# A full block of B21 and B22 in the pairs of chunks: from seventh to third place

## The chip, the cores and the metric

The kernel runs on one core of a Trainium2 chip. The metric is the device time of one execution in microseconds (us); before the change it is 2211.46 us, the median of three runs (2210.63 to 2211.67).

## The reference, cut to what matters

The program is a decoder of two layers on 256 positions of width 2048, all in float32. Each layer has attention, a SwiGLU feed-forward block and a gated embedding. The change is in the feed-forward block:

```python
D_MODEL = 2048; SEQ = 256
D_FF = 5632

def swiglu(h, w1, w3, w2):
    return (jax.nn.silu(h @ w1) * (h @ w3)) @ w2
...
x = x + swiglu(rmsnorm(x, g_ffn[i]), w1[i], w3[i], w2[i])
```

`h` is 256 x 2048, `w1` and `w3` are 2048 x 5632, `w2` is 5632 x 2048.

## The kernel before

**Products.** Every float32 operand is split into a high and a low part in a rounded format (`hi`, `lo` for weights, `st_hi`, `st_lo` for the turned input), and a product is three matmuls: hi by st_hi (L400), lo by st_hi (L401), hi by st_lo (L402). A weight block is loaded by a DMA of the SP queue into `raw` (L112) or, for the blocks spoken of here, into held tiles `r11`, `r12`, `r2` (L105). ScalarE then writes `hi` (L127) and VectorE writes `lo` (L128).

**The stream of blocks.** `WeightStream` keeps one list of all blocks in the order in which TensorE takes them. Each call of `next()` returns the next block and, ahead of that, splits blocks until three full ones are split from the place on; of the small ones only one at a time, since their parts `shi`, `slo` have one buffer each. The full parts have three buffers, so a split waits until TensorE is done with the third full block before it. Splits stay in order on ScalarE and on VectorE (L129 to L131). Behind the split of a small block come its `sums` (L134), additions of held tiles on VectorE, which make the operands of later small blocks. Loads are issued up to two places ahead (L116), each when its buffer is free.

**Pairs of chunks.** The feed-forward block goes over 11 pairs in each layer: a chunk of 512 columns of w1 and the same of w3, in groups of 3, 4 and 4 pairs; after each group its rows of w2 are multiplied. So there are 22 pairs in all, in six groups. The first four k-tiles of a pair are done by a scheme with fewer products (seven instead of eight, with sums of quarters A of the input and B of the weights), the other twelve plainly. A pair takes twelve blocks from the stream; they are named here as in the rest of the text. Small forms, 6 matmuls each: **p1** (B11), **p7** (with the form T3), **p5**, **p6** into `side` tiles, and **q** (the last part of c21). **R** is the full block of B21 and B22, read from `r2`: 6 matmuls into c11 and 6 into c12. Full blocks of four k-tiles, 24 matmuls each: **W1a, W1b, W1c** of w1 into c11 and c21, **W3a, W3b, W3c** of w3 into c12 and c22. The order before is

p1, W1a, p7, W1b, p5, W3a, R, W1c, p6, W3b, q, W3c.

**What else runs.** After p1 ScalarE copies it to `v1` (L493). After p6 VectorE makes v6, v7, v8 (L506 to L509). When c11 and c21 are done, it adds them (L630), ScalarE applies the sigmoid (L632) and VectorE multiplies (L633). When c12 and c22 are done, L636 and L637 run twice each, then two transposes (L325): this is called the tail. The turned result goes into the w2 input by four steps of four copies each, 16 copies `xt` of 32x256 on ScalarE (L330, four are called a move), and a split (`st_hi` L312, `st_lo` L313); these five steps are put off into a list and run one by one at the five calls of `work` inside the next pair (or inside the first w2 chunk, where a group ends). A pair that follows another in its group has them, the first of a group doesn't.

**Order.** Each engine has its own queue, whose order is fixed at compile time: by the order of the text among what that step takes to be ready. Where the trace departs from the text, the trace has the order that ran.

Of the kernel before, what the change touches and what calls it, by code (L numbers as in the profile page):

```python
# [38 lines left out]
CW = 512  # L39
# [4 lines left out]
SN = 2  # L44
# [112 lines left out]
def yoco_kernel(  # L157
# [17 lines left out]
    def cols(w, k0, nk, c0, n, step=4):  # L175

        return [Block(w[(k0 + k) * P:(k0 + min(k + step, nk)) * P, c0:c0 + n].rearrange("(a p) n -> p a n", p=P),
                      min(step, nk - k), n) for k in range(0, nk, step)]

    def pair_cols(wa, ca, wb, cb, nk):  # L180

        def at(w, k, c):
            return w[k * P:(k + SN) * P, c:c + CW].rearrange("(a p) n -> p a n", p=P)

        b11, b21, b12, b22 = at(wa, 0, ca), at(wa, SN, ca), at(wb, 0, cb), at(wb, SN, cb)
        rest = [cols(w, 2 * SN, nk - 2 * SN, c, CW) for w, c in ((wa, ca), (wb, cb))]
        def held(name, a=SN, **more):
            return Block(None, a, CW, held=name, unit=len(blocks), **more)

        return [held("r11", loads=[("r11", [b11])], sums=[("r11", "r12", 0), ("r12", "r2", 1)]), rest[0][0],  # L190
                held("r12", loads=[("r12", [b12]), ("r2", [b21, b22])]), rest[0][1],
                held("r11", sums=[("r11", "r2", 1)]), rest[1][0], held("r2", 2 * SN), rest[0][2],
                held("r11", sums=[("r11", "r2", 0)]), rest[1][1], held("r11"), rest[1][2]]

    IW = IDXN // 3
    FGROUPS = [(0, 3), (3, 7), (7, 11)]
# [27 lines left out]
    stream = WeightStream(tc, raw_pool, half_pool, blocks)  # L224
# [3 lines left out]
    first = const.tile([P, 1], F32, name="first")  # L228
# [76 lines left out]
    def new_station():  # L305
        return (station.tile([P, KT, S], F32R, tag="st_hi", name="st_hi"),
                station.tile([P, KT, S], F32R, tag="st_lo", name="st_lo"))
# [77 lines left out]
    def new_ss():  # L385
        return const.tile([P, NT, NC], F32, tag="ss", name="ss", bufs=2)
# [3 lines left out]
    def work(n):  # L390
        for _ in range(n):
            if bg:
                bg.popleft()()

    def products(st, o, kt, t, h, l, first, last):
        sl = slice(t * P, (t + 1) * P)
        return products_of(st[0][:, kt, sl], st[1][:, kt, sl], o, h, l, first, last)

    def products_of(sh, sl, o, h, l, first, last):
        nc.tensor.matmul(o, sh, h, start=first, stop=False)  # L400
        nc.tensor.matmul(o, sh, l, start=False, stop=False)  # L401
        return nc.tensor.matmul(o, sl, h, start=False, stop=last)  # L402

    def accumulate(st, ktiles, n, acc, pace=(), start=0, end=None, new=None, stop=(True, True)):


        block = 0
        done = start
        while done < (len(ktiles) if end is None else end):
            hi, lo, a = stream.next()  # L410
            for j in range(a):
                kt = ktiles[done + j]
                h, l = hi[:, j * n:(j + 1) * n], lo[:, j * n:(j + 1) * n]
                first, last = done + j == (0 if new is None else start), done + j == len(ktiles) - 1
                for t in range(NT):
                    end_ = products(st, acc[t][:, :n], kt, t, h, l, first and (new is None or new[t]), last and stop[t])
            done += a
            work(pace[block] if block < len(pace) else 0)
            block += 1
        return end_  # L420

    def new_acc():
        return [ps_acc.tile([P, CW], F32, tag="acc", name=f"acc{t}") for t in range(NT)]

    ALL = list(range(KT))
# [7 lines left out]
    class Forms:  # L433
# [20 lines left out]
        def of(self, i):  # L454
            return lambda j: (self.hi[:, i - 1, j, :], self.lo[:, i - 1, j, :])
# [11 lines left out]
    def pair_of_chunks(st, forms, nk, quad):  # L467


        c11, c21, c12, c22 = quad  # L470

        def tiles(k0, t):
            sl = slice(t * P, (t + 1) * P)
            return lambda j: (st[0][:, k0 + j, sl], st[1][:, k0 + j, sl])

        def form(o, of, alone, block=None, at=0):

            hi, lo, _ = stream.next() if block is None else block
            for j in range(SN):
                sl = slice((at + j) * CW, (at + j + 1) * CW)  # L480
                products_of(*of(j), o, hi[:, sl], lo[:, sl], alone in ("alone", "first") and j == 0,
                            alone in ("alone", "last") and j == SN - 1)

        def side_acc(i):
            if i < 2:
                return ps_at.tile([P, CW], F32, tag="at", name=f"side{i}")
            return ps_tr.tile([P, CW], F32, tag="tr", name=f"side{i}")

        ktiles = list(range(nk))
        p1, p5, p6, p7 = (side_acc(i) for i in (0, 2, 3, 1))  # L490
        v1, v6, v7, v8 = (forms.side(n) for n in ("v1", "v6", "v7", "v8"))
        form(p1, tiles(0, 0), "alone")
        nc.scalar.activation(v1, p1, AF.Copy)  # L493
        accumulate(st, ktiles, CW, (c11, c21), (1,), 2 * SN, 2 * SN + 4, new=(True, True))
        form(p7, forms.of(3), "alone")
        work(1)
        accumulate(st, ktiles, CW, (c11, c21), (1,), 2 * SN + 4, 2 * SN + 8)
        form(p5, forms.of(1), "alone")
        work(1)
        accumulate(st, ktiles, CW, (c12, c22), (1,), 2 * SN, 2 * SN + 4, new=(True, True))  # L500
        block = stream.next()
        form(c11, tiles(SN, 0), "more", block)
        form(c12, forms.of(4), "more", block, SN)
        accumulate(st, ktiles, CW, (c11, c21), (), 2 * SN + 8, stop=(True, False))
        form(p6, forms.of(2), "alone")
        nc.vector.tensor_add(v6, v1, p6)  # L506
        nc.vector.tensor_add(v7, v6, p7)
        nc.vector.tensor_sub(v6, v6, p5)
        nc.vector.tensor_sub(v8, v7, p5)  # L509
        accumulate(st, ktiles, CW, (c12, c22), (), 2 * SN + 4, 2 * SN + 8)  # L510
        form(c21, tiles(SN, 1), "last")
        return v1, v7, v6, v8

# [109 lines left out]
    def feed_forward(layer, st, forms, r, ss, nxt, scratch):  # L623
        for gi, (f0, f1) in enumerate(FGROUPS):
            hid = new_station()
            for f in range(f0, f1):
                quad = [ps_acc.tile([P, CW], F32, tag="acc", name=f"acc{j}") for j in range(4)]
                v = pair_of_chunks(st, forms, KT, quad)
                for t in range(NT):
                    nc.vector.tensor_add(v[t], v[t], quad[t])  # L630
                    sg = scratch.tile([P, CW], F32, tag="g", name="sg", bufs=1)
                    nc.scalar.activation(sg, v[t], AF.Sigmoid, scale=r[:, t:t + 1])  # L632
                    nc.vector.scalar_tensor_tensor(v[t], v[t], r[:, t:t + 1], sg, op0=ALU.mult, op1=ALU.mult)  # L633
                accumulate(st, ALL, CW, quad[2:], (), 2 * SN + 8)
                for t in range(NT):
                    nc.vector.tensor_sub(v[2 + t], quad[2 + t], v[2 + t])  # L636
                    nc.vector.scalar_tensor_tensor(v[2 + t], v[2 + t], r[:, t:t + 1], v[t], op0=ALU.mult, op1=ALU.mult)  # L637
                later = []
                ut = transposed_blocks(scratch, v[2:], moves=(1, 1), later=later)
                sl = (slice(None), slice(4 * (f - f0), 4 * (f - f0) + 4), slice(None))  # L640
                bg.extend(later)
                bg.append(lambda ut=ut, sl=sl: split(hid[0][sl], hid[1][sl], ut))
            last = gi == len(FGROUPS) - 1
            for c in range(NC):
                acc = new_acc()
                accumulate(hid, list(range(4 * (f1 - f0))), CW, acc, (3, 2) if c == 0 else ())
                for t in range(NT):
                    xs = x[t][:, c * CW:(c + 1) * CW]
                    nc.vector.tensor_add(xs, xs, acc[t])  # L649
                if last:  # L650
                    square_sum(ss, c, scratch)
                    nxt(c)
# [145 lines left out]
    st = new_station()  # L798
# [49 lines left out]
    with ExitStack() as outer:  # L848
# [3 lines left out]
        ss, st = new_ss(), new_station()  # L852
        forms = Forms(inner)
# [15 lines left out]
        ss, st = new_ss(), new_station()  # L869
# [4 lines left out]
    with tc.tile_pool(name="att1", bufs=1) as pool:  # L874
        kv_st, st = st, new_station()
# [21 lines left out]
    with ExitStack() as outer:  # L897
# [3 lines left out]
        ss, st = new_ss(), new_station()  # L901
        forms = Forms(inner)
# [65 lines left out]
```

## Time and profile before

| | before |
|---|---|
| median of three runs | 2211.46 us |
| profiled execution, its own time | 2210.84 us |
| span of the profiled execution | 2209.1 us |
| TensorE matmuls | 2177.4 us busy, 9780 matmuls |
| VectorE | 1629.6 us busy |
| ScalarE | 1313.7 us busy |
| moved by DMA | 419.23 MB, mean 190 GB/s |
| granted TensorE clock, mean | 0.999 |

How to read it: the span goes from the first to the last instruction of the profiled execution. Matmuls are pipelined and their ends are modelled, so a row of 0.39 us for a matmul overlaps the next one; what counts is the distance from start to start. An idle time is listed with what ended it ("idle before <-releaser").

### The profile page before, as it was taken

How to read it: one execution, taken by the hardware profiler on the slowest of the kernel's cores; microseconds unless marked ns; L12 is line 12 of the kernel's file. 1: busy time of each engine (PE TensorE's matmuls, PEld its weight loads, DVE VectorE, ACT ScalarE, POOL GpSimd, SP SyncE). 2: the span in 40 equal slices, each digit the busy share in tenths (PEclk: the TensorE clock that was granted, in tenths of full speed). 3: DMA queues.
4: the chain of work that ended last, by engine and by line, in shares of the span. 5: the costliest groups of instructions: out<-in, count | busy, mean ns of one | idle time of the engine just before them, and what ended most of it. 6: DMA issues, size and time to landing. Idle time of an engine off the chain costs nothing.

```text
span 2209.1 us, 24961 instructions
## 1 busy us (share of the span) xinstructions
PE 2177.4 (99%) x9780; PEld 1788.8 (81%) x9780; DVE 1629.6 (74%) x1706; ACT 1313.7 (59%) x1676; POOL 39.1 (2%) x38
## 2 busy tenths in 40 slices
PE   9999999999999999999999999999999999999998
PEld 8787788878878887888888778877888888878877
DVE  5877778866887578877777768886678756887764
ACT  5556676644665347666676657675366634676553
POOL 0110000000000000000000000000000000000000
PEclk9999999999999999999999999999999999999999
DMA  7564565656556555555566456556565566546553
GB/s 249 185 191 153 189 201 170 220 183 199 200 181 202 192 187 184 186 189 178 184 212 214 153 172 201 189 182 218 167 224 200 172 209 204 177 162 214 192 190 115
DMA packets 211382, 419.23 MB, mean 190 GB/s; under 512 B 7728, under 2 KB 14512, under 8 KB 211136
## 3 DMA queue, kind: packets, MB, share of 16 engines
q1 hardware_dynamic: 208400, 410.68, 56.1%
q0 software_dynamic: 1248, 4.27, 0.6%
q10 hardware_dynamic: 1616, 2.69, 0.4%
q8 instruction: 76, 1.25, 0.2%
q14 instruction: 42, 0.34, 0.0%
HBM read 415.48 MB, written 2.12 MB: 189 GB/s over the span
## 4 chain that ended last, share of the span: by engine, by line
PE 85%; ACT 7%; DVE 5%; issue 2%; DMA 0%; POOLq 0%; POOL 0%; DVEq 0%; ACTq 0%
PE acc L401 26%; PE acc L402 26%; PE acc L400 26%; ACT xt L330 3%; ACT hi L127 3%; DVE lo L128 2%; PE side L401 2%; PE side L402 1%; PE side L400 1%; PE ps_s L564 1%; PE ps_o L601 1%; DVE slo L128 1%; ACT shi L127 1%; DVE xt L332 1%; PE ps_p L592 0%
## 5 line engine op out<-in xcount | busy, mean ns | idle before, releaser
L400 PE MATMUL acc<-hi,st_hi 128*128 128x512 f32 (+2 forms) x2828 | 1093.0, 387 | 4.2 <-ACT st_hi L312 4.1
L401 PE MATMUL acc<-lo,st_hi 128*128 128x512 f32 (+2 forms) x2828 | 1090.6, 386 | 1.9 <-DVE lo L128 1.7
L402 PE MATMUL acc<-hi,st_lo 128*128 128x512 f32 (+2 forms) x2828 | 1089.1, 385 | 0.0
L128 DVE TENSOR_TENSOR lo<-raw,hi 128x2048 fp32r<-128x2048 f32 (+1 forms) x347 | 795.2, 2293 | 340.2 <-ACT hi L127 339.0
L127 ACT ACTIVATE hi<-raw 128x2048 fp32r<-128x2048 f32 (+1 forms) x347 | 659.1, 1901 | 627.9 <-PE acc L402 514.5
L400 PEld LDWEIGHTS acc<-hi,st_hi 128*128 128x128 f32 x2828 | 530.8, 188 | 112.9 <-ACT st_hi L312 5.3
L401 PEld LDWEIGHTS acc<-lo,st_hi 128*128 128x128 f32 x2828 | 531.2, 188 | 109.5 <-DVE lo L128 4.5
L402 PEld LDWEIGHTS acc<-hi,st_lo 128*128 128x128 f32 x2828 | 531.1, 188 | 106.0 <-issue 2.0
L330 ACT ACTIVATE xt<-xb 32x256 f32<-32x256 f32 x544 | 225.7, 415 | 18.6 <-DVE xb L325 10.2
L128 DVE TENSOR_TENSOR slo<-r,shi 128x1024 fp32r<-128x1024 f32 x110 | 133.7, 1216 | 42.1 <-ACT shi L127 42.0
L127 ACT ACTIVATE shi<-r 128x1024 fp32r<-128x1024 f32 x110 | 115.6, 1051 | 19.5 <-DVE r L134 15.7
L134 DVE TENSOR_TENSOR r<-r,r 128x1024 f32<-128x1024 f32 x88 | 107.5, 1221 | 1.2
L127 ACT ACTIVATE hi<-r 128x2048 fp32r<-128x2048 f32 x22 | 42.2, 1919 | 50.4 <-PE acc L402 50.4
L401 PE MATMUL side<-slo,s_hi 128*128 128x512 f32 x132 | 53.2, 403 | 9.9 <-DVE slo L128 9.9
L128 DVE TENSOR_TENSOR lo<-r,hi 128x2048 fp32r<-128x2048 f32 x22 | 50.2, 2284 | 14.3 <-ACT hi L127 14.3
L506 DVE TENSOR_TENSOR v<-v,side 128x512 f32<-128x512 f32 x22 | 15.1, 688 | 56.2 <-PE side L402 56.2
L332 DVE COPY xt<-xb 32x256 f32<-32x256 f32 x192 | 54.5, 284 | 2.4
L400 PE MATMUL side<-shi,s_hi 128*128 128x512 f32 x132 | 51.7, 392 | 2.5 <-ACT shi L127 2.5
L632 ACT ACTIVATE sg<-v,r_ffn 128x512 f32<-128x512 f32 x44 | 31.5, 717 | 35.2 <-DVE v L633 35.1
L402 PE MATMUL side<-shi,s_lo 128*128 128x512 f32 x132 | 51.6, 391 | 0.0
L578 ACT ACTIVATE sc<-sc,neg 128x128 f32<-128x128 f32 (+1 forms) x64 | 28.3, 444 | 31.2 <-DVE neg L576 31.2
L649 DVE TENSOR_TENSOR x<-x,acc 128x512 f32<-128x512 f32 x48 | 32.8, 688 | 14.4 <-PE acc L402 14.4
(162 smaller groups left out, 1290.4 us busy)
## 6 DMA issues: line engine op xcount, KB each, us to landing
raw<-in_w_dram SPq DMA_DIRECT2D x220, 1024.0 KB, 5.2
r<-in_w_dram SPq DMA_DIRECT2D x88, 512.0 KB, 4.8
raw<-in_w_pg_dram SPq DMA_DIRECT2D x32, 1024.0 KB, 5.1
raw<-in_w_in_a_dram SPq DMA_DIRECT2D x24, 1024.0 KB, 5.4
raw<-in_w_out_a_dram SPq DMA_DIRECT2D x16, 1024.0 KB, 5.1
raw<-in_w_q_b_dram SPq DMA_DIRECT2D x16, 1024.0 KB, 5.1
raw<-in_w_out_b_dram SPq DMA_DIRECT2D x16, 1024.0 KB, 5.1
raw<-in_w_kv_dram SPq DMA_DIRECT2D x8, 1024.0 KB, 5.2
```

Source lines behind the costliest of these rows:

```text
L127: done = (self.nc.scalar.activation(hi[:, :m], raw[:, :m], AF.Copy), self.nc.vector.tensor_sub(lo[:, :m], raw[:, :m], hi[:, :m].bitcast(F32)))
L128: self.nc.vector.tensor_sub(lo[:, :m], raw[:, :m], hi[:, :m].bitcast(F32)))
L134: self.nc.vector.tensor_add(o, o, p)
L330: one = nc.scalar.activation(o, s, AF.Copy)
L332: nc.vector.tensor_copy(o, s)
L400: nc.tensor.matmul(o, sh, h, start=first, stop=False)
L401: nc.tensor.matmul(o, sh, l, start=False, stop=False)
L402: return nc.tensor.matmul(o, sl, h, start=False, stop=last)
L564: nc.tensor.matmul(o, qT[:, h0 + j, t * P:(t + 1) * P], self.kT[:, g, :nk], start=True, stop=True)
L578: nc.scalar.activation(sc[t][:, j, :], sc[t][:, j, :], AF.Exp, bias=neg[:, t, j:j + 1], accum_out=den[:, t, j:j + 1])
L632: nc.scalar.activation(sg, v[t], AF.Sigmoid, scale=r[:, t:t + 1])
L649: nc.vector.tensor_add(xs, xs, acc[t])
```

## The change

The order of the twelve blocks of a pair becomes

p1, W1a, R, p7, W1b, p5, W3a, p6, W1c, q, W3b, W3c.

R goes from seventh to third place; p6 stands ahead of W1c and q behind it, and the last two blocks are W3b and W3c, both after c21 is done. R is now the first to write c12. The loads stay with the third block, and the sums with the first, the p5 and the p6 block; the five calls of `work` stay behind W1a, the third block, W1b, p5 and W3a. Nothing is computed otherwise.

```diff
-        return [held("r11", loads=[("r11", [b11])], sums=[("r11", "r12", 0), ("r12", "r2", 1)]), rest[0][0],
-                held("r12", loads=[("r12", [b12]), ("r2", [b21, b22])]), rest[0][1],
-                held("r11", sums=[("r11", "r2", 1)]), rest[1][0], held("r2", 2 * SN), rest[0][2],
-                held("r11", sums=[("r11", "r2", 0)]), rest[1][1], held("r11"), rest[1][2]]
+        return [held("r11", loads=[("r11", [b11])], sums=[("r11", "r12", 0), ("r12", "r2", 1)]), rest[0][0], held("r2", 2 * SN, loads=[("r12", [b12]), ("r2", [b21, b22])]),
+                held("r12"), rest[0][1], held("r11", sums=[("r11", "r2", 1)]), rest[1][0],
+                held("r11", sums=[("r11", "r2", 0)]), rest[0][2], held("r11"), rest[1][1], rest[1][2]]
...
         accumulate(st, ktiles, CW, (c11, c21), (1,), 2 * SN, 2 * SN + 4, new=(True, True))
+        block = stream.next()
+        form(c11, tiles(SN, 0), "more", block)
+        form(c12, forms.of(4), "first", block, SN)
+        work(1)
         form(p7, forms.of(3), "alone")
-        work(1)
         accumulate(st, ktiles, CW, (c11, c21), (1,), 2 * SN + 4, 2 * SN + 8)
         form(p5, forms.of(1), "alone")
         work(1)
-        accumulate(st, ktiles, CW, (c12, c22), (1,), 2 * SN, 2 * SN + 4, new=(True, True))
-        block = stream.next()
-        form(c11, tiles(SN, 0), "more", block)
-        form(c12, forms.of(4), "more", block, SN)
-        accumulate(st, ktiles, CW, (c11, c21), (), 2 * SN + 8, stop=(True, False))
+        accumulate(st, ktiles, CW, (c12, c22), (1,), 2 * SN, 2 * SN + 4, new=(False, True))
         form(p6, forms.of(2), "alone")
...
-        accumulate(st, ktiles, CW, (c12, c22), (), 2 * SN + 4, 2 * SN + 8)
+        accumulate(st, ktiles, CW, (c11, c21), (), 2 * SN + 8, stop=(True, False))
         form(c21, tiles(SN, 1), "last")
...
-                accumulate(st, ALL, CW, quad[2:], (), 2 * SN + 8)
+                accumulate(st, ALL, CW, quad[2:], (), 2 * SN + 4)
```

## Rows read from the trace of the kernel before

**Rows 1.** The head of the page: the span, and for each engine busy us, share of the span and instructions.

```profile
span 2209.1 us, 24961 instructions
PE 2177.4 (99%) x9780; PEld 1788.8 (81%) x9780; DVE 1629.6 (74%) x1706; ACT 1313.7 (59%) x1676; POOL 39.1 (2%) x38
```

**Rows 2.** The waits of TensorE over the whole span: who waited for whom, us in total, times, the longest in us.

```profile
PE side L401 <- DVE slo L128: 9.9, 16, 0.6
PE acc L400 <- ACT st_hi L312: 4.1, 2, 2.0
PE side L400 <- ACT shi L127: 2.5, 2, 1.3
```

**Rows 3.** Windows, each one pair, from its first matmul to that of the next: the first, second and third pair of the second group of layer 0. After the window its length, then busy us of each engine with its instructions, the granted clock, the share of the DMA engines and GB/s.

```profile
776.72:818.88 42.16, 42.16 (x188) 34.91 (x187) 29.86 (x24) 19.98 (x15) 0.00 (x0) 1.00 0.61 205
818.88:861.98 43.10, 42.48 (x188) 34.84 (x187) 36.11 (x32) 27.81 (x32) 0.00 (x0) 1.00 0.57 195
861.98:905.10 43.12, 42.49 (x188) 34.84 (x187) 36.12 (x32) 27.81 (x32) 0.00 (x0) 1.00 0.54 183
```

**Rows 4.** The timeline of TensorE in the pair that starts at 818.88: start us, us, engine, line, operation, out<-in, count, and idle time before it. The first three lines shown belong to p7, the last two to p5. Twelve matmuls of W1b are left out behind the first line and twelve behind the third; behind the second, three more of p7.

```profile
825.67 0.39 PE L400 MATMUL side<-shi,s_hi 128*128 128x512 f32 x1
...
828.62 0.39 PE L401 MATMUL side<-slo,s_hi 128*128 128x512 f32 x1
...
829.53 0.39 PE L402 MATMUL side<-shi,s_lo 128*128 128x512 f32 x1
...
832.48 0.39 PE L400 MATMUL side<-shi,s_hi 128*128 128x512 f32 x1
833.49 0.50 PE L401 MATMUL side<-slo,s_hi 128*128 128x512 f32 x1 [0.62 <-DVE slo L128]
```

**Rows 5.** The timeline of ScalarE in the same pair: `hi` of W1b, `shi` of p7, the copy of v1, `hi` of R, two moves, `shi` of p5, the third move, `hi` of W1c, and `shi` of p6.

```profile
819.08 1.92 ACT L127 ACTIVATE hi<-raw 128x2048 fp32r<-128x2048 f32 x1 [1.12 <-PE acc L402]
822.03 1.06 ACT L127 ACTIVATE shi<-r 128x1024 fp32r<-128x1024 f32 x1 [1.03 <-DVE r L134]
822.99 0.58 ACT L493 ACTIVATE v<-side 128x512 f32<-128x512 f32 x1
825.88 1.92 ACT L127 ACTIVATE hi<-r 128x2048 fp32r<-128x2048 f32 x1 [2.30 <-PE acc L402]
827.70 3.39 ACT L330 ACTIVATE xt<-xb 32x256 f32<-32x256 f32 x8
831.12 1.06 ACT L127 ACTIVATE shi<-r 128x1024 fp32r<-128x1024 f32 x1
832.20 1.69 ACT L330 ACTIVATE xt<-xb 32x256 f32<-32x256 f32 x4
833.91 1.92 ACT L127 ACTIVATE hi<-raw 128x2048 fp32r<-128x2048 f32 x1
...
837.57 1.06 ACT L127 ACTIVATE shi<-r 128x1024 fp32r<-128x1024 f32 x1
```

**Rows 6.** The timeline of VectorE in the same pair: the second sum of p1's split in the tail of the pair before, `lo` of W1b, the second transpose; `slo` of p5; and around the additions after p6, with `lo` of the next pair's W1a and `slo` of q.

```profile
820.04 0.69 DVE L636 TENSOR_TENSOR v<-acc,v 128x512 f32<-128x512 f32 x1
820.64 1.22 DVE L134 TENSOR_TENSOR r<-r,r 128x1024 f32<-128x1024 f32 x1
...
824.29 2.29 DVE L128 TENSOR_TENSOR lo<-raw,hi 128x2048 fp32r<-128x2048 f32 x1
826.49 0.71 DVE L325 STREAM_TRANSPOSE xb<-v 128x512 f32<-128x512 f32 x1
...
832.21 1.22 DVE L128 TENSOR_TENSOR slo<-r,shi 128x1024 fp32r<-128x1024 f32 x1 [1.70 <-ACT shi L127]
...
849.93 0.69 DVE L506 TENSOR_TENSOR v<-v,side 128x512 f32<-128x512 f32 x1 [2.56 <-PE side L402]
850.54 2.29 DVE L128 TENSOR_TENSOR lo<-raw,hi 128x2048 fp32r<-128x2048 f32 x1
852.74 0.68 DVE L507 TENSOR_TENSOR v<-v,side 128x512 f32<-128x512 f32 x1
853.34 1.22 DVE L128 TENSOR_TENSOR slo<-r,shi 128x1024 fp32r<-128x1024 f32 x1
```

**Rows 7.** The timeline of VectorE at the end of the first group of layer 0: a tail with nothing in it.

```profile
450.32 1.28 DVE L636 TENSOR_TENSOR v<-acc,v 128x512 f32<-128x512 f32 x2
451.52 1.41 DVE L637 SCALAR_TENSOR_TENSOR v<-v,r_ffn,v 128x512 f32<-128x512 f32 x2
452.84 1.30 DVE L325 STREAM_TRANSPOSE xb<-v 128x512 f32<-128x512 f32 x2
```

**Rows 8.** The DMA issues on the page, the loads of held tiles: count, KB each, median us from issue to landing.

```profile
r<-in_w_dram SPq DMA_DIRECT2D x88, 512.0 KB, 4.8
```

**Rows 9.** The timeline of the SP queue in the pair that starts at 818.88: the two loads into `r2` for the next pair.

```profile
842.19 0.88 SPq L105 DMA_DIRECT2D r<-in_w_dram  x2
```

**Rows 10.** The timeline of ScalarE in the first pair of layer 0, which starts at 320.68 (scaling of the turned x, `shi` of p7), and at the end of the first group of that layer (three moves, a `hi`, the fourth move, `st_hi`).

```profile
328.23 1.71 ACT L462 ACTIVATE xt<-xt,gT 128x256 f32<-128x256 f32 x4
329.85 1.04 ACT L127 ACTIVATE shi<-r 128x1024 fp32r<-128x1024 f32 x1
...
454.18 5.12 ACT L330 ACTIVATE xt<-xb 32x256 f32<-32x256 f32 x12 [1.50 <-DVE xb L325]
459.32 1.92 ACT L127 ACTIVATE hi<-raw 128x2048 fp32r<-128x2048 f32 x1
461.26 1.69 ACT L330 ACTIVATE xt<-xb 32x256 f32<-32x256 f32 x4
462.99 1.06 ACT L312 ACTIVATE st_hi<-xt 128x1024 fp32r<-128x1024 f32 x1
```

## The prediction, made before the changed kernel was run

> **What bounds the kernel now.** I read the page's busy times first, then the waits of TensorE, then the three windows of one pair each, then the timelines of TensorE, ScalarE, VectorE and the SP queue inside one pair. TensorE is busy 2177.4 of 2209.1 us [rows 1]; the reader should not conclude that nothing can be had, but that whatever can be had is a wait of TensorE. The list of its waits has only one that recurs in the pairs: a matmul of a `side` tile that waits for `slo`, 16 times; two more come twice each [rows 2]. The windows say what it costs: the first pair of a group takes 42.16 us with TensorE busy throughout, the next two take 43.10 and 43.12 [rows 3]. A pair has 186 matmuls (six full blocks of 24, R with 12, five small forms of 6), so 42.16 / 186 = 0.2267 us is the undisturbed step: 1.36 us for a form, 5.44 for a full block, 2.72 for R. There are 22 pairs, in six groups; 22 − 6 = 16 pairs follow another pair, and 16 is the count of the waits. So about 0.95 us per following pair, 16 × 0.95 = 15.2 us, is lost at one place; the idle time alone is 9.9 us [rows 2], since the listed gap of 0.62 us [rows 4] begins only where the last matmul's modelled end lies and leaves out slower steps behind it.
>
> The place is p5. I count t from the pair's first matmul at 818.88. p7's first matmul runs at t = 6.79, then twelve matmuls of W1b come in between, and the other five of p7 run from 9.74 to 10.9 [rows 4]; the order fixed at compile time has split p7, because `slo` of p7 comes late: VectorE still had the two sums of p1's split between L636 and the transposes, then `lo` of W1b [rows 6]. p5 starts at t = 13.60, only 2.7 us after p7 ends, and `shi`/`slo` have one buffer: `shi` of p5 can't start before p7 has ended. It starts later still, at t = 12.24, because ScalarE first runs eight copies `xt` (3.39 us) of the pair before [rows 5]. `slo` follows at 13.33 and takes 1.22 [rows 6]; TensorE resumes at 14.61 [rows 4].
>
> **The change part by part.** Nothing is added or removed: the same 186 matmuls, splits, four sums and loads per pair. In the new order the undisturbed pair starts its parts at: p1 0, W1a 1.36, R 6.80, p7 9.52, W1b 10.88, p5 16.32, W3a 17.68, p6 23.12, W1c 24.48, q 29.92, W3b 31.28, W3c 36.72, end 42.16. Following `next()` by hand (three full blocks ahead, one small one), the splits are called in this order: W1b, p7, W3a, W1c, p5, W3b, p6, W3c, q, W1a', p1', R' (a prime is the next pair). A full split waits until TensorE has left the third full block before it: W3a for W1a, W1c for R, W3b for W1b, W3c for W3a, R' for W3b, W1b' for W3c.
>
> *p7.* Its sums now belong to a split that is called one block earlier (before W3b), so they leave the tail. The tail alone (two each of L636, L637 and transposes) takes 3.8 us where nothing stands in it [rows 7]. `shi` of p7 follows `hi` of W1b (0.2 to 2.1) and the copy of v1: done at 3.8. `slo` at the latest after the tail, `lo` of W1b (2.29) and itself (1.22): t = 7.0. It is wanted at 9.75. p7 is no longer split, so p5 has a whole W1b, 5.44 us, behind p7 instead of 2.7.
>
> *p5.* This decides. New is that `hi` of W1c stands between the copies and `shi` of p5. ScalarE: `hi` of W3a from 7.0 (as `hi` of R now, 0.2 after W1a ends [rows 5]) to 8.9; four copies, a move, 1.69, to 10.5; `hi` of W1c 1.92 to 12.4; `shi` 1.06 to 13.4. VectorE: `lo` of W1c 12.5 to 14.8, `slo` of p5 to 16.0. Wanted: 16.32 + 0.23 = 16.55. So there is no wait, with 0.55 us to spare, if the first move stands ahead of `hi` of W3a. If it starts at 5.8 and pushes `hi` of W3a to 7.5, the margin is about 0.15 us. If both moves stand behind `hi` of W3a, as they do now [rows 5], everything is 1.7 us later: `slo` ends at 17.7 and TensorE loses 1.2 us. I take the first: now the transposes end at 826.49 + 0.71, t = 8.3, after `hi` of R became possible at 7.0; without the two sums (1.22 each [rows 6]) they end at 3.5 to 5.8 (the upper end with `lo` of W1b ahead of the second one, as in [rows 6]), when ScalarE has nothing else until 6.8.
>
> ScalarE and VectorE do not overtake here: `shi` of p5 waited out the copies although its buffer was free from t = 11.0 [rows 4, 5]. The Trainium skill (TensorE: Matmul & The Clock Gate, the table at its head) gives both engines a strict first-in, first-out queue; that speaks against this change, which puts one more `hi` ahead of p5's `shi`. By that rule the bad order costs what rival C says; were it otherwise, `shi` would run at 11.1 in any order and only my forecast would remain. This trace agrees with the page, by the 831.12 of [rows 5].
>
> *p6 and q.* p6's `shi` follows `hi` of W3b (16.5 to 18.4) and a move (to 20.1); `slo` ends at 22.4, wanted at 23.35. q follows p6 by one full block, as it follows it now: today `slo` of q ends 4.63 us after L506 starts (849.93 to 853.34 + 1.22 [rows 6]); from p6's end at 24.48 plus 0.2 this is 29.3, wanted at 30.15. Should all four additions stand ahead of `lo` of W3c, it is 1.2 later and 0.4 is lost.
>
> *c12, the tail, the loads.* c12 is first written at 8.16 instead of 14.96; its reader of the pair before, L636, starts at 1.16 even in today's crowded order [rows 6]. c21 ends two blocks ahead of the pair's end instead of one, which only gives the sigmoid more room. R' is split at 36.9 instead of in the next pair, and the sums want r12' and r2' at about 36 instead of 43. The SP queue issues r2' when the last sum has read r2: now at 842.19, t = 23.3 [rows 9]; then after p6's `slo`, `st_lo` and the sum, at most 25.0. Two loads at 4.8 us each to landing [rows 8], issued 0.4 apart, are there by 31: the spare falls from some 14 us to 5 and costs nothing; without it VectorE would stand. The raw load of W1b' behind them in that queue is issued by 26 and wanted at 42.4.
>
> *Where the trace gives only bounds.* The first pair of a layer waits at p7 for `shi`, behind the turning of x (the 328.23 copies, `shi` from 329.85 [rows 10]; 1.3 us idle, twice [rows 2]). p7 is then due at 320.68 + 9.52 = 330.2 and `shi` ends at 330.9: 0.7 to 1.5 us saved at best, but `hi` of W1c now stands ahead of p5's `shi` there too, and that can lose 1.3. I take 0 for the two, bounds −3 and +2.6. The wait at the end of each layer's first group (twice 2.0 [rows 2]) hangs on three moves, a `hi`, the fourth move and `st_hi` in series after the last pair's tail [rows 10]; the order there is untouched: 0, bounds −0.8 and +0.4.
>
> *The sum.* 2210.84 us, the profiled execution (span 2209.1), less 15.2 is 2195.6; the median of the runs shown is 0.62 above it: **2196.3 us**.
>
> **The rivals.** *B, a small wait stays.* The margin of 0.15 at p5 is missed, or the additions push q: 0.3 to 0.6 us in each of 16 pairs, 5 to 10 back: 2201 to 2206, say 2203. For it: margins of 0.15 to 0.8 us are thin against sums of ten durations. Against: each was worked out in the less favourable order, and q's pattern is already in the trace.
>
> *C, slower.* Both moves stand behind `hi` of W3a. Then p5 loses 1.2 us plus the 0.1 of the slower restart, 1.3 instead of 0.95: 16 × 0.35 = +5.5 us, 2217. It decides from the point where the second transpose ends after t = 6.8. For it: that is today's order [rows 5]. Against: the two sums that made it so are gone, and 5.8 leaves a microsecond.
>
> *D, the change does not do what it says.* The compile-time order splits p7 or p5 around W1b again and the same 2.7 us remains ahead of the next form: 2211. Against: p7's `slo` has 2.7 us to spare.
>
> **How the numbers follow.** Forecast 0.66 (2193 to 2200 with the bounds above), B 0.14, C 0.11, D 0.09. The range 2193 to 2207 takes forecast and B, 8 in 10. A run here can tell about 0.2% (4.4 us) from no change, so faster means below 2207: forecast and nearly all of B, 0.78; same is D with a rest of B, 0.12; slower is C with its thinner cases counted as same, 0.10.
>
> **What would show it.** Right: the 16 waits of `side` for `slo` gone, following pairs at 42.2 us in the windows, p7 in one run of six matmuls, a move ahead of `hi` of W3a on ScalarE. B: a wait of a few tenths at p5 or q. C: eight copies behind `hi` of W3a and a p5 wait above 0.9. Wrong in a way that I have not costed: VectorE waiting for an r2 load at p1', or p5 waiting in the first pairs of groups, where no moves are.

## The result, and the profile after

The changed kernel takes 2195.48 us, the median of four runs (2195.25 to 2196.21), against 2211.53 us for the kernel before on the same chip (four runs, 2210.63 to 2211.67): a ratio of 0.9927, 95% interval 0.9915 to 0.9938, 16 us or 0.73% faster. The forecast was 2196.3.

| | before | after |
|---|---|---|
| median | 2211.53 us | 2195.48 us |
| span of the profiled execution | 2209.1 us | 2193.7 us |
| TensorE matmuls | 9780 | 9780 |
| waits of `side` for `slo` | 16, 9.9 us | 2, 0.6 us |

In the changed kernel's listing the matmul lines are one lower (L399 to L401), `xt` is L329, the transposes L324, and the tail is L634 and L635. The waits of TensorE over the span, answering to [rows 2] (us in total, times, longest; three of seven lines, the other four are as they were within 0.1 us):

```profile
PE acc L399 <- ACT st_hi L311: 3.8, 2, 1.9
PE side L399 <- ACT shi L127: 1.2, 2, 0.6
PE side L400 <- DVE slo L128: 0.6, 2, 0.3
```

The 16 waits are gone; the two for `slo` that are listed now stand in the first pair of each layer, where the kernel before had none. The windows of the three pairs of [rows 3], and as the fourth the first pair of layer 0:

```profile
771.94:814.10 42.16, 42.16 (x187) 34.91 (x186) 32.72 (x27) 19.98 (x15) 0.00 (x0) 1.00 0.59 200
814.10:856.26 42.16, 42.16 (x187) 34.91 (x186) 36.19 (x32) 27.65 (x32) 0.00 (x0) 1.00 0.61 200
856.26:898.42 42.16, 42.16 (x187) 34.91 (x186) 36.19 (x32) 27.61 (x32) 0.00 (x0) 1.00 0.57 188
320.72:364.48 43.76, 42.88 (x188) 34.67 (x186) 37.69 (x40) 28.71 (x33) 0.72 (x1) 1.00 0.58 192
```

A following pair now takes what the first of a group takes, 42.16 us, with TensorE busy throughout: it has no wait left to take out. 16 × 0.95 = 15.2 us is nearly the whole difference of the spans, 15.4.

Why shows on ScalarE, in the pair that starts at 814.10, answering to [rows 5]: `hi` of W1b, v1, `shi` of p7, the first move, `hi` of W3a, the second move, `hi` of W1c, `shi` of p5.

```profile
814.30 1.92 ACT L127 ACTIVATE hi<-raw 128x2048 fp32r<-128x2048 f32 x1 [3.52 <-PE acc L401]
816.13 0.58 ACT L492 ACTIVATE v<-side 128x512 f32<-128x512 f32 x1
816.60 1.05 ACT L127 ACTIVATE shi<-r 128x1024 fp32r<-128x1024 f32 x1
817.57 1.70 ACT L329 ACTIVATE xt<-xb 32x256 f32<-32x256 f32 x4
821.10 1.92 ACT L127 ACTIVATE hi<-raw 128x2048 fp32r<-128x2048 f32 x1 [1.84 <-PE acc L401]
823.04 1.70 ACT L329 ACTIVATE xt<-xb 32x256 f32<-32x256 f32 x4
824.77 1.92 ACT L127 ACTIVATE hi<-raw 128x2048 fp32r<-128x2048 f32 x1
826.59 1.04 ACT L127 ACTIVATE shi<-r 128x1024 fp32r<-128x1024 f32 x1
```

And on VectorE, answering to [rows 6]: the tail, `lo` of W1b, `slo` of p7; `lo` of W1c and `slo` of p5; the first addition after p6 (L504 here) and `slo` of q; then, at the end of the pair, p1's two sums and `lo` of R for the next one.

```profile
813.62 1.37 DVE L634 TENSOR_TENSOR v<-acc,v 128x512 f32<-128x512 f32 x2 [0.25 <-PE acc L401]
814.91 1.40 DVE L635 SCALAR_TENSOR_TENSOR v<-v,r_ffn,v 128x512 f32<-128x512 f32 x2
816.24 1.30 DVE L324 STREAM_TRANSPOSE xb<-v 128x512 f32<-128x512 f32 x2
817.46 2.25 DVE L128 TENSOR_TENSOR lo<-raw,hi 128x2048 fp32r<-128x2048 f32 x1
819.63 1.21 DVE L128 TENSOR_TENSOR slo<-r,shi 128x1024 fp32r<-128x1024 f32 x1
...
826.72 2.29 DVE L128 TENSOR_TENSOR lo<-raw,hi 128x2048 fp32r<-128x2048 f32 x1 [1.38 <-ACT hi L127]
828.93 1.22 DVE L128 TENSOR_TENSOR slo<-r,shi 128x1024 fp32r<-128x1024 f32 x1
...
838.79 0.68 DVE L504 TENSOR_TENSOR v<-v,side 128x512 f32<-128x512 f32 x1
...
842.19 1.22 DVE L128 TENSOR_TENSOR slo<-r,shi 128x1024 fp32r<-128x1024 f32 x1
...
850.85 2.48 DVE L134 TENSOR_TENSOR r<-r,r 128x1024 f32<-128x1024 f32 x2
853.25 2.28 DVE L128 TENSOR_TENSOR lo<-r,hi 128x2048 fp32r<-128x2048 f32 x1
```

The sums (850.85) are over before the tail starts (855.8 for the next pair), so the tail runs without a break, its transposes end at t = 3.4, and the first move starts at t = 3.5, ahead of `hi` of W3a. In [rows 5] both moves stand behind the `hi` of that place. `slo` of p5 ends at 830.15, t = 16.05; TensorE takes it at 830.65, t = 16.55, without a wait:

```profile
830.42 0.39 PE L399 MATMUL side<-shi,s_hi 128*128 128x512 f32 x1
830.65 0.39 PE L400 MATMUL side<-slo,s_hi 128*128 128x512 f32 x1
```

### The profile page after: what moved, and what is told of

Same layout as the page of the kernel before. It is cut to its first block, busy times and chain, and to the rows that moved or that the text cites. A ratio compares the mean times of both kernels' runs of the same rounds, so it can differ in the third digit from the quotient of the medians.

```text
span 2193.7 us, 24969 instructions
## 1 busy us (share of the span) xinstructions
PE 2173.4 (99%) x9780; PEld 1790.1 (82%) x9780; DVE 1630.2 (74%) x1706; ACT 1310.0 (60%) x1676; POOL 39.0 (2%) x38
## 4 chain that ended last, share of the span: by engine, by line
PE 92%; DVE 4%; ACT 3%; issue 1%; POOLq 0%; POOL 0%; DVEq 0%; ACTq 0%
PE acc L400 27%; PE acc L401 27%; PE acc L399 27%; PE side L400 2%; PE side L401 2%; PE side L399 2%; DVE lo L128 2%; PE ps_s L562 1%; ACT hi L127 1%; PE ps_o L599 1%; ACT xt L329 1%; DVE xt L331 1%; PE ps_p L590 0%; PE ps_i L755 0%; PE emb L399 0%
## 5 line engine op out<-in xcount | busy, mean ns | idle before, releaser
L399 PE MATMUL acc<-hi,st_hi 128*128 128x512 f32 (+2 forms) x2828 | 1092.8, 387 | 3.8 <-ACT st_hi L311 3.8
L401 PE MATMUL acc<-hi,st_lo 128*128 128x512 f32 (+2 forms) x2828 | 1089.0, 385 | 0.0
L399 PEld LDWEIGHTS acc<-hi,st_hi 128*128 128x128 f32 x2828 | 530.9, 188 | 111.6 <-ACT st_hi L311 5.0
L401 PEld LDWEIGHTS acc<-hi,st_lo 128*128 128x128 f32 x2828 | 531.0, 188 | 106.3 <-issue 2.0
L329 ACT ACTIVATE xt<-xb 32x256 f32<-32x256 f32 x544 | 226.1, 416 | 17.9 <-DVE xb L324 9.2
L127 ACT ACTIVATE hi<-r 128x2048 fp32r<-128x2048 f32 x22 | 42.2, 1920 | 36.8 <-PE acc L401 36.8
L399 PE MATMUL side<-shi,s_hi 128*128 128x512 f32 x132 | 51.6, 391 | 1.2 <-ACT shi L127 1.2
L401 PE MATMUL side<-shi,s_lo 128*128 128x512 f32 x132 | 51.4, 389 | 0.0
L374 ACT ACTIVATE sq<-x 128x512 f32<-128x512 f32 x54 | 33.4, 619 | 13.2 <-DVE x L679 12.0
```

The lines of the kernel that those rows point to most:

```text
L127: done = (self.nc.scalar.activation(hi[:, :m], raw[:, :m], AF.Copy), self.nc.vector.tensor_sub(lo[:, :m], raw[:, :m], hi[:, :m].bitcast(F32)))
L329: one = nc.scalar.activation(o, s, AF.Copy)
L374: nc.scalar.activation(sq, x[t][:, c * CW:(c + 1) * CW], AF.Square, accum_out=ss[:, t, c:c + 1])
```

## The experiments

The change has two halves: R goes to third place, and the end of the pair is reordered so that two full blocks stand behind q. Only the second takes p1's split, and its sums, out of the tail. **Theory S** says that this alone is the gain; its rivals give it to the distance that R puts ahead of p7 (D, another one than the D of the prediction), to the time behind p7 (E), or say that the place of the copies does not matter (F).

**The end alone** (`end_only`), from the kernel before:

```diff
-                held("r11", sums=[("r11", "r2", 1)]), rest[1][0], held("r2", 2 * SN), rest[0][2],
-                held("r11", sums=[("r11", "r2", 0)]), rest[1][1], held("r11"), rest[1][2]]
+                held("r11", sums=[("r11", "r2", 1)]), rest[1][0], held("r2", 2 * SN),
+                held("r11", sums=[("r11", "r2", 0)]), rest[0][2], held("r11"), rest[1][1], rest[1][2]]
...
-        accumulate(st, ktiles, CW, (c11, c21), (), 2 * SN + 8, stop=(True, False))
         form(p6, forms.of(2), "alone")
...
-        accumulate(st, ktiles, CW, (c12, c22), (), 2 * SN + 4, 2 * SN + 8)
+        accumulate(st, ktiles, CW, (c11, c21), (), 2 * SN + 8, stop=(True, False))
...
-                accumulate(st, ALL, CW, quad[2:], (), 2 * SN + 8)
+                accumulate(st, ALL, CW, quad[2:], (), 2 * SN + 4)
```

> Only the second half of the change: R stays in seventh place, but q stands ahead of both W3b and W3c as in the new order (p1, W1a, p7, W1b, p5, W3a, R, p6, W1c, q, W3b, W3c). Theory S (the two sums of p1's split in VectorE's tail make the moves late and pull p7 apart; taking them out of the tail is what helped): the sums come one block earlier here too, the first move runs at about t = 3.5, p7 runs in one piece, slo of p5 ends near 12.9 and is wanted at 13.8, so no wait at p5: following pairs 42.2 us, 2195 to 2197 us in all. Rival D (distance: it is R between W1a and p7, which gives p7 2.7 us more, that helped): p7 and p5 stand as in the kernel before, 0.95 us per following pair remain, 2210 to 2212 us.

Measured: 2196.15 us, ratio to the kernel before 0.9927 (0.9912 to 0.9942), the whole gain with R still in seventh place. The second pair of its second group in the windows, and ScalarE in that pair (the first move, `hi` of R, the second move, `shi` of p5):

```profile
814.76:856.92 42.16, 42.16 (x187) 34.91 (x186) 36.27 (x32) 27.73 (x32) 0.00 (x0) 1.00 0.60 200
```

```profile
818.22 1.70 ACT L330 ACTIVATE xt<-xb 32x256 f32<-32x256 f32 x4
821.76 1.92 ACT L127 ACTIVATE hi<-r 128x2048 fp32r<-128x2048 f32 x1 [1.84 <-PE acc L402]
823.70 1.70 ACT L330 ACTIVATE xt<-xb 32x256 f32<-32x256 f32 x4
825.43 1.06 ACT L127 ACTIVATE shi<-r 128x1024 fp32r<-128x1024 f32 x1
```

Its `slo` of p5 ends at 827.75 and is used at 828.59: 0.84 us to spare, more than the 0.5 of the changed kernel: there p5 comes 2.7 us later in the pair, but with `hi` and `lo` of W1c ahead of them its `shi` and `slo` come 3.1 us later. Rival D is out.

**R in third place alone** (`third_only`), from the changed kernel, with the end of the pair of before:

```diff
-                held("r11", sums=[("r11", "r2", 0)]), rest[0][2], held("r11"), rest[1][1], rest[1][2]]
+                rest[0][2], held("r11", sums=[("r11", "r2", 0)]), rest[1][1], held("r11"), rest[1][2]]
...
+        accumulate(st, ktiles, CW, (c11, c21), (), 2 * SN + 8, stop=(True, False))
         form(p6, forms.of(2), "alone")
...
-        accumulate(st, ktiles, CW, (c11, c21), (), 2 * SN + 8, stop=(True, False))
+        accumulate(st, ktiles, CW, (c12, c22), (), 2 * SN + 4, 2 * SN + 8)
...
-                accumulate(st, ALL, CW, quad[2:], (), 2 * SN + 4)
+                accumulate(st, ALL, CW, quad[2:], (), 2 * SN + 8)
```

> Only the first half of the change: R in third place, but the end of the pair as before (p1, W1a, R, p7, W1b, p5, W3a, W1c, p6, W3b, q, W3c), so p1's split and its two sums are called behind q again and lie in the tail. Theory S: the second transpose ends near t = 8.3, both moves stand behind hi of W3a, slo of p5 ends near 17.7 where 16.55 is wanted: a wait of 1.0 to 1.2 us plus 0.1 in each of 16 following pairs, 2195.5 + 16 x 1.1 to 1.3 = 2213 to 2216 us, slower than the kernel before. Rival D: R in third place is the gain, 2195 to 2197 us.

Measured: 2213.8 us, ratio 1.0007 (0.9997 to 1.0016) to the kernel before, no gain at all. A following pair in the windows, the tail with a sum in it on VectorE, and p5 on TensorE:

```profile
819.11:862.35 43.24, 42.50 (x188) 34.83 (x186) 35.94 (x32) 27.70 (x32) 0.00 (x0) 1.00 0.60 195
```

```profile
820.28 0.68 DVE L635 TENSOR_TENSOR v<-acc,v 128x512 f32<-128x512 f32 x1
820.88 1.22 DVE L134 TENSOR_TENSOR r<-r,r 128x1024 f32<-128x1024 f32 x1
...
826.73 0.71 DVE L324 STREAM_TRANSPOSE xb<-v 128x512 f32<-128x512 f32 x1
...
835.51 1.22 DVE L128 TENSOR_TENSOR slo<-r,shi 128x1024 fp32r<-128x1024 f32 x1
```

```profile
835.43 0.39 PE L399 MATMUL side<-shi,s_hi 128*128 128x512 f32 x1
835.66 0.39 PE L399 MATMUL acc<-hi,st_hi 128*128 128x512 f32 x1
836.79 0.50 PE L400 MATMUL side<-slo,s_hi 128*128 128x512 f32 x1 [0.74 <-DVE slo L128]
837.13 0.40 PE L401 MATMUL side<-shi,s_lo 128*128 128x512 f32 x1
```

The second transpose ends at t = 8.3, as in the kernel before, and the rest follows: `slo` of p5 ends at t = 17.6. p7 runs in one piece here and a whole W1b lies between it and p5, and the wait is there all the same.

**The last link by itself** (`move_later`), the kernel before with one call of `work` moved from behind p7 to behind p5. The steps leave their list in order, so the second move now runs at the call behind W1b, and the third and the fourth at the two behind p5; the expectation speaks of the second alone:

```diff
         form(p7, forms.of(3), "alone")
-        work(1)
...
         form(p5, forms.of(1), "alone")
-        work(1)
+        work(2)
```

> The kernel before, with the order of its blocks untouched; only the second move is put off from behind p7 to behind p5, where two are run then. Theory S in its last link (it is the copies ahead of shi of p5 on ScalarE that cost): p7 is pulled apart as before and ends at t = 11.0, but ScalarE is free by 10.5, shi of p5 runs at 11.2 to 12.3, slo ends at 13.5, wanted at 13.83: no wait, 2195 to 2198 us. Rival E (2.7 us behind p7's end is too short for shi and slo in any case): some 0.5 us or more of the wait remain, 2204 to 2211 us.

Measured: 2196.97 us, ratio 0.9930 (0.9915 to 0.9945). On ScalarE one move is left ahead of `shi` of p5, which now waits for p7's last matmul and for nothing else; the third line is `slo` of p5 on VectorE:

```profile
823.14 1.68 ACT L330 ACTIVATE xt<-xb 32x256 f32<-32x256 f32 x4
825.40 1.06 ACT L127 ACTIVATE shi<-r 128x1024 fp32r<-128x1024 f32 x1 [0.58 <-PE side L402]
826.49 1.23 DVE L128 TENSOR_TENSOR slo<-r,shi 128x1024 fp32r<-128x1024 f32 x1 [0.55 <-ACT shi L127]
```

This `slo` ends at 827.72 and is used at 828.14, and the pair takes 42.16 us. With p7 still pulled apart, 2.7 us behind it is enough for `shi` and `slo`, if ScalarE is free: rival E is out. One call of `work` taken out and one made a 2 do what the change does.

**The first link by itself** (`no_sums`), the kernel before with p1's two sums left out, so that it computes something else and only its time is of use:

```diff
-        return [held("r11", loads=[("r11", [b11])], sums=[("r11", "r12", 0), ("r12", "r2", 1)]), rest[0][0],
+        return [held("r11", loads=[("r11", [b11])], sums=[]), rest[0][0],
```

> The kernel before without the two sums behind p1's split (r11 + r12 and r12 + r22 are left out, so p7, p5, p6 and q multiply other weights; everything else is as before). Theory S: the tail is free of them, the transposes end 2.4 us earlier, near t = 5.9, the first move runs ahead of hi of R, p7 is pulled apart by less, and p5 finds its slo: 2195 to 2198 us. Rival D (distance): the order of the blocks is that of before and so is the time, 2209 to 2212 us.

Measured: 2196.11 us, ratio 0.9928 (0.9911 to 0.9944). In the pair that starts at 814.16 the first move now stands ahead of `hi` of R on ScalarE, with the order of the blocks untouched:

```profile
818.04 1.70 ACT L330 ACTIVATE xt<-xb 32x256 f32<-32x256 f32 x4 [0.34 <-DVE xb L325]
821.16 1.92 ACT L127 ACTIVATE hi<-r 128x2048 fp32r<-128x2048 f32 x1 [1.42 <-PE acc L402]
```

The sums are 2.4 us of VectorE per pair, an engine that is idle for 7.0 of the 43.10 us of such a pair [rows 3]; `end_only` still has them, outside the tail, and loses nothing. Where they stand costs TensorE 0.95.

**The copies back in the bad place** (`moves_behind`), the changed kernel with p7, the sums and the tail as they are:

```diff
-        accumulate(st, ktiles, CW, (c11, c21), (1,), 2 * SN, 2 * SN + 4, new=(True, True))
+        accumulate(st, ktiles, CW, (c11, c21), (), 2 * SN, 2 * SN + 4, new=(True, True))
...
-        work(1)
+        work(2)
         form(p7, forms.of(3), "alone")
```

> The changed kernel with its block order, sums and tail untouched; only the first move is called together with the second, behind R, so that both stand behind hi of W3a on ScalarE (the condition of rival C of the prediction). Theory S in its last link: ScalarE runs hi of W3a from 7.0, eight copies to 12.2, hi of W1c to 14.1, shi of p5 to 15.1; slo ends at 17.6 to 17.7 instead of 16.05, wanted at 16.55: about 1.1 us per following pair, 2195.5 + 16 x 1.1 = 2213 us. Rival F (p7 in one piece and a whole W1b behind it are enough, wherever the copies stand): 2195 to 2197 us.

Measured: 2213.83 us, ratio to the kernel before 1.0012 (1.0003 to 1.0021): all is lost again. ScalarE and then TensorE in the pair that starts at 819.13:

```profile
826.13 1.92 ACT L127 ACTIVATE hi<-raw 128x2048 fp32r<-128x2048 f32 x1 [3.45 <-PE acc L401]
827.95 3.40 ACT L329 ACTIVATE xt<-xb 32x256 f32<-32x256 f32 x8
831.37 1.92 ACT L127 ACTIVATE hi<-raw 128x2048 fp32r<-128x2048 f32 x1
833.19 1.04 ACT L127 ACTIVATE shi<-r 128x1024 fp32r<-128x1024 f32 x1
```

```profile
836.80 0.50 PE L400 MATMUL side<-slo,s_hi 128*128 128x512 f32 x1 [0.74 <-DVE slo L128]
```

Rival F is out, and this is rival C of the prediction with its price: 0.74 us listed idle, 43.23 us per pair.

**What is left** was tried at two of the places that the waits still name, the `st_hi` behind a layer's first group and the first pair of a layer. First, all five steps at once behind the first w2 block (`five_at_once`, from the changed kernel):

```diff
-                accumulate(hid, list(range(4 * (f1 - f0))), CW, acc, (3, 2) if c == 0 else ())
+                accumulate(hid, list(range(4 * (f1 - f0))), CW, acc, (5,) if c == 0 else ())
```

> The changed kernel, and the five steps put off (four moves and the split) all run behind the first block of the first w2 chunk of a group, instead of three and then two. At the end of the first group of a layer the fourth move and st_hi then stand ahead of the hi (1.92 us) that stood between the third and the fourth move: the wait of TensorE for st_hi, 2.05 us and 0.1 of slower restart, goes down by about 1.9 in each of the two layers: 2195.5 - 3.8 = 2191.7 us. Rival: the hi that is now later (needed one block after) takes its place and nothing is gained, 2195.5 us.

Measured: 2195.38 us, ratio to the kernel before 0.9928 (0.9915 to 0.9940): nothing against the changed kernel. The wait for `st_hi` fell from 1.9 to 0.2 us, and one for the `hi` that had been put behind the copies took its place:

```profile
460.29 0.73 PE L399 MATMUL acc<-hi,st_hi 128*128 128x512 f32 x2 [1.24 <-ACT hi L127]
461.25 0.50 PE L399 MATMUL acc<-hi,st_hi 128*128 128x512 f32 x1 [0.22 <-ACT st_hi L311]
```

The same 16 copies and that `hi` are in series on ScalarE in either order; my expectation of 2191.7 had the `hi` due a block later than it is, and its rival came true. Second, the scaling of the last turned chunk of x on VectorE as well (`both_ends`), and then that edit alone (`scale_on_vector`):

```diff
-            nc.scalar.activation(xt[:, j, :], xt[:, j, :], AF.Copy, scale=gT[:, at:at + 1])
+            if c == NC - 1:
+                nc.vector.tensor_scalar(xt[:, j, :], xt[:, j, :], gT[:, at:at + 1], None, op0=ALU.mult)
+            else:
+                nc.scalar.activation(xt[:, j, :], xt[:, j, :], AF.Copy, scale=gT[:, at:at + 1])
```

> As the run before, and in the first pair of a layer the four scalings of the last turned chunk of x run on VectorE, which is idle there for 3 us, instead of ScalarE (1.71 us just ahead of shi of p7). The pair of 43.76 us should come down toward 42.2 in both layers: 2191.7 - 2 x 0.8 to 1.5 = 2189 to 2190 us. Rival: on ScalarE shi of p7 runs no earlier, since v1 and the copies ahead of it set its time, and VectorE's scalings push slo: 2191 to 2193 us.

> The changed kernel with only the four scalings of the last turned chunk of x on VectorE, the five steps behind w2 as in the changed kernel. If the first pair of a layer (42.83 us in the run with both edits, 43.76 in the changed kernel) is the whole of that run's gain, as the traces say, this run gives the same 2195.5 - 2 x 0.93 = 2193.6 us, and the five steps at once are worth nothing. Otherwise it stays at 2195.

Measured: 2194.06 us, ratio 0.9921 (0.9907 to 0.9934), with both edits; 2194.18 us, ratio 0.9918 (0.9904 to 0.9932), with the scaling alone. The 2189 to 2190 expected of both edits was missed, since the five steps at once give nothing and the first pair of a layer comes down to 42.84 us, not to 42.2. The intervals overlap with the changed kernel's, so the times alone don't settle a gain of 1.3 us; the traces show where it would be, in the first pair of each layer, whose waits for `shi` and `slo` are no longer in the list. With the scaling alone the pair in layer 0, 43.76 us in the changed kernel, is:

```profile
319.97:362.81 42.84, 42.80 (x188) 34.76 (x186) 38.73 (x44) 26.99 (x29) 0.72 (x1) 1.00 0.59 196
```

Last, the 16 copies of the last pair of each group shared between ScalarE and VectorE, with the scaling and the five steps at once (`shared_moves`; the copies on VectorE are held behind the last `lo` as those on ScalarE are behind the last `hi`):

```diff
-                ut = transposed_blocks(scratch, v[2:], moves=(1, 1), later=later)
+                ut = transposed_blocks(scratch, v[2:], moves=(0, 1) if f == f1 - 1 else (1, 1), later=later)
```

> The run scale_on_vector, and in the last pair of each group half of the 16 copies run on VectorE (idle there for 6.7 us) and the five steps all stand behind the first w2 block. ScalarE then has 8 copies (3.4 us) instead of 16 (6.8), so hi of the following w2 block can run right when its buffer is free and st_hi still ends 2 to 3 us earlier: of the 2.05 us that TensorE waits at the end of the first group, 1.5 to 2.0 go in each layer: 2193.6 - 3.0 to 4.2 = 2189.4 to 2190.6 us. Rival: st_lo on VectorE is now pushed behind lo of that block and takes over the wait, 2192 to 2194 us.

Measured: 2190.77 us, ratio 0.9903 (0.9889 to 0.9916), the fastest of all, 4.7 us below the changed kernel by medians of different comparisons, and just above the 2189.4 to 2190.6 expected; the two intervals barely meet. ScalarE at the end of the first group, and what TensorE still waits for there:

```profile
450.69 3.41 ACT L329 ACTIVATE xt<-xb 32x256 f32<-32x256 f32 x8 [1.34 <-DVE xb L324]
454.13 1.92 ACT L127 ACTIVATE hi<-raw 128x2048 fp32r<-128x2048 f32 x1
455.95 1.04 ACT L311 ACTIVATE st_hi<-xt 128x1024 fp32r<-128x1024 f32 x1
```

```profile
PE acc L401 <- DVE st_lo L312: 1.7, 2, 0.8
```

`st_hi` no longer waits, and `st_lo` has taken over a part, as its rival said: 0.8 instead of 1.9 us in each layer.

## Why the prediction was right, point by point

**The size.** The sum had one term, 16 following pairs at 0.95 us. The windows give 43.10 and 43.12 before and 42.16 after; the forecast was 0.8 us above the measured median. No wait at p5 or q is listed in a following pair, so rival B did not come, and p7 runs in one piece (823.62 to 824.76), so neither did the prediction's D.

**p7.** Foreseen: the sums leave the tail, `slo` of p7 at t = 7.0 at the latest. Measured: 819.63 + 1.21 − 814.10 = 6.74. That the sums leave the tail carried the result, as `end_only` (2196.15) and `third_only` (2213.8) show. That p7 begins 2.7 us later and is no longer split, which the prediction put beside it, did not: `third_only` and `moves_behind` have both and lose the gain, `move_later` has neither and keeps it. One name was wrong: the `hi` at 819.08 [rows 5] and the `lo` at 824.29 [rows 6] are W3a's, not W1b's, for W1b's matmuls use their `lo` from 826.13 on, and this one ends at 826.58. The times in the sum don't depend on it.

**p5.** Foreseen: `slo` at t = 16.0 with the first move ahead of `hi` of W3a, 0.55 us to spare. Measured: 16.05 and 0.5. The condition was the right one: `moves_behind` broke it and nothing else, and lost the gain.

**What R's move is worth.** The prediction didn't say that the two halves could be told apart, and gave R's move a part in the gain that it does not have. R in third place brings an extra `hi` ahead of `shi` of p5 and takes 0.3 us of its margin; the gain comes with the end of the pair alone, or, just as well, with one move put off in the kernel before.

**q, p6, the loads.** `slo` of q ends 842.19 + 1.22 − 838.79 = 4.62 us after the first addition starts, foreseen 4.63. The loads of the next r2 are issued at t = 24.8, foreseen at most 25.0, and `hi` of R at 851.02 waited for TensorE, not for them.

**The places given as bounds.** The first pair of a layer went from 43.71 to 43.76 us: 0.6 us idle instead of 1.3 at p7's `shi`, the rest given back at p7's `slo` (0.3 idle) and in slower restarts; at p5, where up to 1.3 was allowed for, no idle is listed. 0 was the value taken. The wait at the end of the first group stayed: 1.9 instead of 2.0.

**Rival C was oversized.** It was priced at 1.3 us per pair, 2217. `moves_behind` and `third_only` had it at 1.07 (43.23 − 42.16), 2213.8: the compile-time order there puts one matmul of W3a between p5's first two, which covers 0.23 us. So this order is 16 × (1.07 − 0.95) = 1.9 us slower than the kernel before, not 5.5; the two runs show 2.5 and 1.6 by medians.

## What to carry to other kernels

Where the engine that sets the time is busy nearly throughout, list its waits by place and count; a count that equals the number of some repeated stage gives the size of the prize before any change is thought of. Then follow the late operand back over the other engines' queues to the first instruction that stands ahead of it without need: here two additions on VectorE delayed transposes, these put eight copies behind a `hi` instead of around it on ScalarE, and only then TensorE waited. Any link can be cut, and the cheapest edit may be another than the one at hand.

## What was not expected of the hardware

A wait here cost more than its listed idle time, and the runs show the parts; the prediction had named them from [rows 4] and put the slower restart at 0.1. In `third_only` 0.74 us listed idle make 43.24 − 42.16 = 1.08 us of a pair. The list counts from the modelled end of the row before (835.66 + 0.39 = 836.05), while an undisturbed step would have started at 835.89: 0.16 us. The matmul that resumes has a row of 0.50 us instead of 0.39, and the next one starts 0.34 us later (836.79 to 837.13) instead of 0.23: 0.11. The rest, 0.07, lies in steps slightly above 0.23 us behind it. Adding up listed idle times (9.9 us) would have forecast only two thirds of the gain.
